# Matmul operands at the same place modulo 512 bytes of SBUF

## The chip, the cores and the metric

The kernel runs on one core of a Trainium2 chip. The metric is the time of one execution on the device, in microseconds (us).

## The reference

One layer of a streaming encoder over 512 tokens of 1024 features, in float32: a half ffn, a mixer with three attention branches, a second half ffn, and a last norm.

```python
x = x + 0.5 * swiglu(rmsnorm(x, ffn1_norm), ffn1_wg, ffn1_wu, ffn1_wd)      # D 1024, D_FF 2816
h = rmsnorm(x, mix_norm)
proj = h @ w_in                      # q, k, v of branches a and b, q of branch c
...                                  # a: differential attention, b: banded, c: into 256 memory tokens
gates = sigmoid(h @ w_gate + b_gate)
y = sum over branches of (o_i @ w_branch[i]) * gates[i]
x = x + y @ w_out
x = x + 0.5 * swiglu(rmsnorm(x, ffn2_norm), ffn2_wg, ffn2_wu, ffn2_wd)
x = rmsnorm(x, final_norm)
swiglu(h, wg, wu, wd) = (silu(h @ wg) * (h @ wu)) @ wd
```

## The kernel before

**Products in three terms.** Every large product is made of float32 operands that are split into a high and a low part of type fp32r (`split`, L75): ScalarE casts the high part (L77), VectorE subtracts (L78). A product is then three matmuls, high with high, high with low, low with high (`mm3`, L108, or `mm7`, L345). The names of the parts end in h and l, or hi and lo. A matmul has a stationary operand (lhsT, 128 columns of 512 bytes in each partition, loaded by a weight load of its own) and a moving one (rhs, 256, 384 or 512 columns). In the rows of the profile a matmul reads `ps_s<-mhi,whi`: it writes ps_s, its moving operand is mhi, its stationary one whi.

**The ffns.** The up products (`mm7`, L354) are made with seven combined products per pair of weight tiles in place of eight: the tokens are combined once into M1 to M7 (`Operands`, tiles mhi and mlo), the weight blocks are combined as they arrive (`Item.prep`). A product is 24 matmuls of 256 columns: M moving, a weight block stationary. Weight blocks stand in a ring of six (`block`, L339): four of them in whi and wlo, two in fhi and flo. The gated results stand in gh and gl. In the down products they are stationary and the weight blocks moving, 512 columns each (`mm3` at L110 to L112). `run_jobs` lays out the order of the products and of the weight blocks that are split ahead of them.

**The mixer.** h2 (hh and hl) is the normed input, transposed. In the units' projections (`proj_rows`, 384 columns) and in those of c and of the memory, it or the memory's mh and ml is stationary, and the weights move; in the gates (`gate`) the weights are stationary (fh and fl) and h2 moves, in the branches (`branch`) oT (oah, obh, och and their low parts) moves. The scores read qk and kx, the products with the probabilities read vt and pT. The order of the work on TensorE is written out by hand (the PLAN strings); a scheduler with a model of time orders the other engines.

**Places in SBUF.** Pools stack their tiles from the bottom of each partition up; pools with side="right" stack from the top down, which is at byte 229344, 480 bytes over a multiple of 512. The pool base lies below all others; its last tiles are many of 32 bytes (`tiny`), and the tile le of 32 bytes (L619). mhalf is 8 columns that hold -0.5, of which GpSimd reads at most the first four (L121). Nearly all operand tiles have a length that is a multiple of 512 bytes, so that the rest of a tile's place modulo 512 is that of all its slices of 128 columns. The rests of the operands that the large products read:

| product | matmuls, columns | moving | its rest before | stationary | its rest before | both after |
|---|---|---|---|---|---|---|
| ffns, up | 2496 x 256 | M (mhi, mlo) | 480 | whi, wlo | 32 | 32 |
| ffns, up | 1200 x 256 | M | 480 | fhi, flo | 64 | 32 |
| ffns, down | 720 x 512 | whi, wlo | 32 | gh, gl | 64 | 32 |
| ffns, down | 336 x 512 | fhi, flo | 64 | gh, gl | 64 | 32 |
| gates | 576 x 512 | hh, hl | 480 | fh, fl | 160 | 32 |
| branches | 288 x 512 | oah, obh, och, ... | 64 | fh, fl | 160 | 32 |
| units' projections | 768 x 384 | whi, wlo | 32 | hh, hl | 480 | 32 |
| projections of c | 96 x 512 | whi, wlo | 32 | hh, hl | 480 | 32 |
| projections of the memory | 96 x 512 | mwh, mwl | 64 | mh, ml | 480 | 32 |
| output product | 192 x 512 | whi, wlo, kx, w4 | 32 | yh, yl | 64 | 32 |
| scores of the units | 128 x 256 to 512 | qk, kx | 64, 32 | qk | 64 | 32 |

Of the kernel before, what the change touches and what calls it, by code (L numbers as in the profile page):

```python
# [11 lines left out]
F32 = mybir.dt.float32  # L12
# [6 lines left out]
P = 128  # L19
# [28 lines left out]
def layer_kernel(ctx: ExitStack, tc: tile.TileContext, a: dict, out: bass.AP):  # L48
    nc = tc.nc

    base = ctx.enter_context(tc.tile_pool(name="base", bufs=1))
# [19 lines left out]
    def buf4k(name):  # L71

        return base.tile([P, 1024], F32, tag="raw", name=name, bufs=6)
# [18 lines left out]
    def load(src, n):  # L92

        raw = buf4k("wraw")[:, :n]
        dst = raw
        if len(src.shape) == 3:
            dst = raw.rearrange("p (a b) -> p a b", a=src.shape[1])
        nc.sync.dma_start(out=dst, in_=src)
        return raw
# [30 lines left out]
    def load_gain(name):  # L130
        g = scratch("gain")
        nc.sync.dma_start(out=g, in_=a[name].partition_broadcast(P))
        return g[:, :512], g[:, 512:]
# [29 lines left out]
    def right_pool(name):  # L163
        return tc.tile_pool(name=name, bufs=1, side="right", reuse_waits="tile")
# [6 lines left out]
    def new_M(pool):  # L171
        mh, ml = (pool.tile([P, 7, 4, HS], F32R, name=n) for n in ("mhi", "mlo"))
        return {i: (mh[:, i - 1], ml[:, i - 1]) for i in range(1, 8)}
# [59 lines left out]
    def squares(src):  # L233
# [4 lines left out]
            square_half(src[:, d], dump[:, d], ss[:, dh:dh + 1])  # L238
        return ss

    Mp = right_pool("M1")
    M1 = new_M(Mp.__enter__())
    memp = tc.tile_pool(name="memp", bufs=1, reuse_waits="tile")
# [7 lines left out]
    for t in range(NT):  # L251
        nc.sync.dma_start(out=x_sb[:, t, :], in_=x_v[:, t, :])
        if t == 0:
            gain1 = load_gain("ffn1_norm")
        elif t < 3:
            w1_raw.append(load(a["ffn1_w1"][0, t - 1], 1024))

    ident = base.tile([P, P], F32, name="ident")
    make_identity(nc, ident)
# [2 lines left out]
    mhalf = base.tile([P, 8], F32, name="mhalf")  # L262
# [353 lines left out]
    nc.sync.dma_start(out=la, in_=a["a_lambda"].rearrange("(u v) d -> u v d", u=2).partition_broadcast(P))  # L616
    lp = heads(lam[:, 256:384], 2)
    nc.vector.tensor_tensor(out=lp, in0=la[:, :, 0, :], in1=la[:, :, 1, :], op=ALU.mult)
    le = base.tile([P, 4], F32, name="le")  # L619
    nc.vector.tensor_reduce(out=le[:, 0:2], in_=lp, axis=AX.X, op=ALU.add)  # L620
    nc.scalar.activation(out=le[:, 0:2], in_=le[:, 0:2], func=AF.Exp)
    nlam = le[:, 2:3]
# [14 lines left out]
    mo = mix_o.__enter__()  # L637
    mix = tc.tile_pool(name="mix", bufs=1, reuse_waits="tile")
    mp = mix.__enter__()


    def bcast(name, src, n):
# [485 lines left out]
```

## Time and profile before

| | |
|---|---|
| median of 3 runs | 1273.69 us (1273.66 to 2465.04) |
| the profiled execution | 1273.05 us, of which 1271.3 us from the first to the last instruction (the span) |
| granted TensorE clock, mean | 0.987 |
| TensorE matmuls (PE) | busy 1232.4 us, 97% of the span, 7808 instructions |
| weight loads (PEld) | busy 1116.9 us, 88%, 7808 |
| VectorE (DVE) | busy 842.8 us, 66% |
| ScalarE (ACT) | busy 596.8 us, 47% |
| GpSimd (POOL) | busy 107.1 us, 8% |
| read from HBM | 122.11 MB, 99 GB/s over the span |

The busy times are those of one execution. Matmuls overlap: one starts while the one before it is still in the array, so the duration of a matmul in a row (276 to 397 ns here) is longer than the distance between two starts. That distance is read from the starts in the timeline, or from a row of the chain that merges many matmuls of one kind.

### The profile page before, as it was taken

What the parts mean: (1) busy time and instruction counts of PE and PEld (TensorE: products, weight loads), DVE (VectorE), ACT (ScalarE), POOL (GpSimd) and SP (SyncE); (2) the same over time, 40 slices, a digit from 0 to 9 for tenths busy, and PEclk for the clock granted to TensorE, in tenths of its full rate; (3) what the DMA queues carried; (4) which work ended last, traced back from release to release, by engine and by line L of the source; (5) the groups of instructions that cost most, each with busy time, mean ns of one, the idle gap of its engine ahead of it and who ended that gap; (6) DMA issues with size and microseconds to landing.
All of it is one profiled execution on the core that took longest, in us unless ns stands there. A gap on an engine that the chain in (4) does not pass through costs nothing.

```text
span 1271.3 us, 19657 instructions
## 1 busy us (share of the span) xinstructions
PE 1232.4 (97%) x7808; PEld 1116.9 (88%) x7808; DVE 842.8 (66%) x1377; ACT 596.8 (47%) x1115; POOL 107.1 (8%) x108
## 2 busy tenths in 40 slices
PE   7799999999998999999999999999979999999997
PEld 7789989989986799999999999888878998998996
DVE  7977667667564756766765565453697766766753
ACT  7535425435443446554555454443463452543543
POOL 1100000000000301111221121020000000000002
PEclk8899999999999899999999999999989999999999
DMA  5533324322334403321222320254133242342311
GB/s 215 174 108 116 115 71 128 113 91 101 116 118 130 109 28 108 88 67 58 88 87 70 89 83 31 75 159 160 34 127 122 76 133 91 101 129 73 130 35 67
DMA packets 53084, 127.57 MB, mean 100 GB/s; under 512 B 10112, under 2 KB 10624, under 8 KB 52992
## 3 DMA queue, kind: packets, MB, share of 16 engines
q1 hardware_dynamic: 52416, 125.27, 30.9%
q8 instruction: 61, 1.00, 0.3%
q10 hardware_dynamic: 576, 1.05, 0.2%
q14 instruction: 31, 0.25, 0.1%
HBM read 122.11 MB, written 4.19 MB: 99 GB/s over the span
## 4 chain that ended last, share of the span: by engine, by line
PE 90%; DVE 4%; DMA 2%; ACT 1%; POOL 1%; issue 1%; SPq 0%; POOLq 0%; ACTq 0%; DVEq 0%
PE ps_s L354 19%; PE ps_g L110 9%; PE ps_g L112 9%; PE ps_g L111 9%; PE ps_o L354 5%; PE ps_p L110 4%; PE ps_p L354 4%; PE ps_p L111 4%; PE ps_p L112 4%; PE ps_g L354 4%; PE ps_s L110 2%; PE ps_s L112 2%; PE ps_s L111 2%; PE ps_o L881 2%; PE ps_s L849 2%; PE ps_t L697 1%
## 5 line engine op out<-in xcount | busy, mean ns | idle before, releaser
L77 ACT CAST whi<-wraw 128x1024 fp32r<-128x1024 f32 (+1 forms) x120 | 119.0, 993 | 141.3 <-PE ps_s L354 68.6
L78 DVE TENSOR_TENSOR wlo<-wraw,whi 128x1024 fp32r<-128x1024 f32 (+1 forms) x120 | 137.9, 1151 | 65.6 <-ACT whi L77 64.6
L354 PE MATMUL ps_s<-mhi,whi 128*128 128x256 f32 x496 | 138.3, 279 | 2.3 <-ACT snap L397 2.0
L354 PE MATMUL ps_s<-mlo,whi 128*128 128x256 f32 x496 | 137.7, 278 | 0.0
L354 PE MATMUL ps_s<-mhi,wlo 128*128 128x256 f32 x496 | 136.8, 278 | 0.0
L77 ACT CAST whi<-quarter 128x1024 fp32r<-128x1024 f32 x54 | 56.7, 1051 | 91.8 <-PE ps_s L354 22.7
L354 PEld LDWEIGHTS ps_s<-mhi,whi 128*128 128x128 f32 x496 | 93.8, 189 | 4.1 <-ACT snap L397 2.8
L110 PE MATMUL ps_p<-whi,hh 128*128 128x384 f32 (+1 forms) x264 | 94.8, 359 | 0.0
L354 PEld LDWEIGHTS ps_s<-mlo,whi 128*128 128x128 f32 x496 | 93.7, 189 | 1.0 <-DVE mlo L78 0.2
L354 PEld LDWEIGHTS ps_s<-mhi,wlo 128*128 128x128 f32 x496 | 93.2, 189 | 0.0
L112 PE MATMUL ps_p<-whi,hl 128*128 128x384 f32 (+1 forms) x264 | 89.2, 338 | 0.0
L111 PE MATMUL ps_p<-wlo,hh 128*128 128x384 f32 (+1 forms) x264 | 89.2, 338 | 0.0
L78 DVE TENSOR_TENSOR wlo<-quarter,whi 128x1024 fp32r<-128x1024 f32 x54 | 65.9, 1221 | 24.5 <-ACT whi L77 24.5
L110 PE MATMUL ps_g<-hh,fh 128*128 128x512 f32 x192 | 78.4, 408 | 0.0
L112 PE MATMUL ps_g<-hh,fl 128*128 128x512 f32 x192 | 75.8, 395 | 0.0
L111 PE MATMUL ps_g<-hl,fh 128*128 128x512 f32 x192 | 75.7, 394 | 0.0
L834 DVE CAST kx<-ps_t 128x256 fp32r<-128x256 f32 x32 | 13.6, 425 | 83.7 <-PE ps_t L832 83.7
L121 POOL TENSOR_TENSOR rsh<-msh,mhalf 128x4 f32<-128x4 f32 x38 | 45.2, 1191 | 276.9 <-DVE msh L127 225.2
L78 DVE TENSOR_TENSOR fl<-wraw,fh 128x768 fp32r<-128x768 f32 x48 | 50.0, 1042 | 26.1 <-ACT fh L77 26.1
L77 ACT CAST fhi<-quarter 128x1024 fp32r<-128x1024 f32 x34 | 35.5, 1049 | 59.1 <-PE ps_s L354 16.4
L354 PE MATMUL ps_s<-mhi,fhi 128*128 128x256 f32 x208 | 59.2, 285 | 2.5 <-ACT fhi L77 2.5
L354 PE MATMUL ps_s<-mlo,fhi 128*128 128x256 f32 x208 | 58.9, 283 | 0.0
(376 smaller groups left out, 3662.8 us busy)
## 6 DMA issues: line engine op xcount, KB each, us to landing
wraw<-in_ffn_w SPq DMA_DIRECT2D x88, 512.0 KB, 4.0
wraw<-in_ffn_wd SPq DMA_DIRECT2D x44, 512.0 KB, 3.9
wraw<-in_w_u SPq DMA_DIRECT2D x32, 384.0 KB, 3.3
wraw<-in_w_gb SPq DMA_DIRECT2D x32, 384.0 KB, 3.0
wraw<-in_w_gf SPq DMA_DIRECT2D x16, 384.0 KB, 3.1
wraw<-in_w_mem_kv SPq DMA_DIRECT2D x8, 512.0 KB, 4.1
wraw<-in_w_out SPq DMA_DIRECT2D x8, 512.0 KB, 4.5
x_sb<-in_x SPq DMA_DIRECT2D x4, 512.0 KB, 7.0
```

The costliest lines, as they stand in the source:

```text
L77: nc.scalar.copy(out=hi, in_=raw)
L78: (engine or nc.vector).tensor_tensor(out=lo, in0=raw, in1=f32(hi), op=ALU.subtract)
L110: nc.tensor.matmul(ps, lhsT=st[0], rhs=mv[0], start=first, stop=False)
L111: nc.tensor.matmul(ps, lhsT=st[0], rhs=mv[1], start=False, stop=False)
L112: return nc.tensor.matmul(ps, lhsT=st[1], rhs=mv[0], start=False, stop=last)
L121: nc.gpsimd.tensor_tensor(out=rs, in0=ms, in1=mhalf[:, :n], op=ALU.pow)
L354: nc.tensor.matmul(ps[:, c], lhsT=x, rhs=y, start=first and j + k + n == 0, stop=k == 3 and n == 2, skip_group_check=True)
L697: nc.tensor.transpose(ps[:, j * P:(j + 1) * P], pt[:, j * P:(j + 1) * P], ident)
L834: nc.vector.tensor_copy(out=un.kx[:, :, qs], in_=heads(p2[:, 0:256], 2))
L849: nc.tensor.matmul(out_, lhsT=q, rhs=k, start=j == 0, stop=j == 1)
L881: nc.tensor.matmul(o[:, vs], lhsT=pT[:, j * P:(j + 1) * P], rhs=un.v[:, j, vs], start=j == 0, stop=j == i)
```

## The change

Two pads and a merged tile move the places of tiles; nothing else changes. A pad of 112 words (448 bytes) at the top of the right side, entered before M1, lowers all tiles of that side by 448 bytes: their rest goes from 480 to 32. The tile le is now columns 4 to 8 of mhalf, which makes base shorter by 32 bytes: the rest of the tiles that stand above it goes from 64 to 32. A pad of 104 words (416 bytes) behind the small tables of the pool mix moves the tiles behind it (vt, the score tiles, fh and fl, pT and others) from 160 to 32. The empty lines of the diff do nothing.

```diff
+    ctx.enter_context(right_pool("pad")).tile([P, 112], F32, name="pad")
     Mp = right_pool("M1")
     M1 = new_M(Mp.__enter__())
...
     nc.vector.tensor_tensor(out=lp, in0=la[:, :, 0, :], in1=la[:, :, 1, :], op=ALU.mult)
-    le = base.tile([P, 4], F32, name="le")
+    le = mhalf[:, 4:8]
     nc.vector.tensor_reduce(out=le[:, 0:2], in_=lp, axis=AX.X, op=ALU.add)
...
     mp = mix.__enter__()
+
+
+    mp.tile([P, 104], F32, name="pad")
```

Engine by engine the built program has the same instructions in the same order, with the same waits on the same values; only the name le has become mhalf in its three writers and 16 readers. The tiles that stand below le in base (x_sb, the raw weights, ident, whi and wlo, w4 and kx) keep their places. In the after kernel all operands of the table have rest 32; the stationary operands of the transposes get rest 32 or 288, and ident, which moves in them, stays at 128.

## Rows read from the trace of the kernel before

**Rows 1.** The page, part 4: the chain of waits, shares of the span.

```profile
PE 90%; DVE 4%; DMA 2%; ACT 1%; POOL 1%; issue 1%; SPq 0%; POOLq 0%; ACTq 0%; DVEq 0%
```

**Rows 2.** Windows: us, busy us (instructions) of each engine, clock, DMA share, GB/s.

```profile
66.00:372.00 306.00, 305.19 (x2107) 281.20 (x2106) 212.62 (x255) 133.47 (x192) 1.65 (x3) 1.00 0.33 105
...
456.00:805.00 349.00, 348.72 (x2097) 318.91 (x2096) 221.94 (x610) 183.09 (x496) 60.63 (x59) 1.00 0.24 74
...
938.00:1190.00 252.00, 249.55 (x1762) 231.73 (x1761) 181.86 (x209) 107.89 (x147) 0.00 (x0) 1.00 0.35 111
```

**Rows 3.** The chain of waits in time: start us, us, what.

```profile
1025.43 2.88 PE ps_g L354 x24
1028.31 2.73 PE ps_s L354 x24
```

**Rows 4.** Timeline of PE, second ffn: first matmuls of two blocks.

```profile
1025.26 0.28 PE L354 MATMUL ps_g<-mhi,fhi 128*128 128x256 f32 x1
...
1028.14 0.28 PE L354 MATMUL ps_s<-mhi,whi 128*128 128x256 f32 x1
```

**Rows 5.** Timeline of all engines, second ffn: a matmul, the next weight load.

```profile
1025.98 0.28 PE L354 MATMUL ps_g<-mhi,fhi 128*128 128x256 f32 x1
1025.99 0.19 PEld L354 LDWEIGHTS ps_g<-mlo,fhi 128*128 128x128 f32 x1
```

**Rows 6.** Source L354, ffns, up: count, ns min/median/max, first and last start.

```profile
L354 PE MATMUL ps_s<-mhi,whi x496: 275/276/562, 16.4 to 1235.9; 128*128 128x256 f32 x166
...
L354 PE MATMUL ps_s<-mhi,fhi x208: 277/283/582, 40.5 to 1219.4; 128*128 128x256 f32 x104
```

**Rows 7.** Tile gh, ffns, down: the same columns.

```profile
L110 PE MATMUL ps_g<-whi,gh x120: 392/396/476, 66.2 to 1263.6; 128*128 128x512 f32 x120
...
L110 PE MATMUL ps_s<-fhi,gh x28: 387/390/504, 77.9 to 1239.9; 128*128 128x512 f32 x28
```

**Rows 8.** Timeline of PE, first ffn, down: from whi to fhi.

```profile
255.66 0.40 PE L112 MATMUL ps_o<-whi,gl 128*128 128x512 f32 x1
...
256.60 0.39 PE L110 MATMUL ps_s<-fhi,gh 128*128 128x512 f32 x1
...
258.66 0.39 PE L110 MATMUL ps_s<-fhi,gh 128*128 128x512 f32 x1
...
261.84 0.39 PE L112 MATMUL ps_p<-fhi,gl 128*128 128x512 f32 x1
```

**Rows 9.** Source L78, VectorE's subtraction in a split: columns as above.

```profile
L78 DVE TENSOR_TENSOR wlo<-quarter,whi x54: 1215/1220/1227, 39.3 to 1210.3; 128x1024 fp32r<-128x1024 f32 x54
...
L78 DVE TENSOR_TENSOR flo<-quarter,fhi x34: 1215/1224/1226, 43.0 to 1212.6; 128x1024 fp32r<-128x1024 f32 x34
```

**Rows 10.** Source L111, the third term of other products: columns as above.

```profile
L111 PE MATMUL ps_p<-wlo,hh x264: 332/336/398, 372.6 to 787.9; 128*128 128x384 f32 x128, 128*128 128x512 f32 x4
L111 PE MATMUL ps_g<-hl,fh x192: 387/395/399, 433.9 to 865.9; 128*128 128x512 f32 x192
...
L111 PE MATMUL ps_s<-mwl,mh x32: 391/394/629, 394.8 to 430.7; 128*128 128x512 f32 x32
...
L111 PE MATMUL ps_g<-oal,fh x32: 392/397/401, 644.4 to 791.4; 128*128 128x512 f32 x32
...
L111 PE MATMUL ps_s<-wlo,yh x16: 392/396/398, 846.7 to 910.8; 128*128 128x512 f32 x16
```

**Rows 11.** Waits of TensorE: waiter, awaited, us in total, times, longest.

```profile
PE ps_o L354 <- ACT whi L77: 7.3, 2, 3.7
PE ps_s L110 <- DVE mk L580: 5.6, 1, 5.6
```

**Rows 12.** Windows, one stretch at a lower clock: columns of rows 2.

```profile
412.72:419.54 6.82, 5.57 (x14) 4.33 (x15) 5.00 (x11) 1.19 (x2) 2.67 (x4) 0.50 0.33 113
```

**Rows 13.** Groups by shape, scores of the units: count, busy us, mean ns, idle.

```profile
L849 PE MATMUL ps_s<-qk 128*128 128x256 f32 x32 | 8.3, 281 | 0.0
...
L849 PE MATMUL ps_s<-qk 128*128 128x512 f32 x16 | 6.3, 394 | 0.0
```

## The prediction

> **What bounds the kernel now.** I read the page first. TensorE is busy for 97% of the span (the table above), and the chain of waits runs through it for 90% [rows 1]. The windows by stage show where: in the first ffn (66 to 372 us), the mixer (456 to 805 us) and most of the second ffn (938 to 1190 us) TensorE is busy for all but 0.3 to 2.5 us, while VectorE, the next engine, stands at 64 to 72% [rows 2]. In these stretches the time is the number of matmuls times the distance from one matmul's start to the next one's. I call that distance the pitch. So the question is what the pitch depends on.
>
> The chain of waits shows it. It merges each product of an ffn into one row of 24 matmuls. All these blocks do the same work, 256 moving columns of M against a weight block, yet some rows last 2.73 us and others 2.88 us [rows 3]. The timeline says which is which: the block of 2.88 us reads its weight block from fhi and flo, the next one, of 2.73 us, from whi and wlo [rows 4]. Per matmul that is 120 ns against 113.7 ns. The two kinds differ in nothing but the place of the stationary operand. M begins at rest 480 (modulo 512 bytes), whi at 32, fhi at 64.
>
> The timeline with both parts of TensorE says how one operand's place can touch the other: the load of the next matmul's weights starts 0.01 us after the running matmul does [rows 5]. So the two read SBUF side by side, from the matmul's first column on. The source view of that line gives the same difference as duration, median 276 ns with whi and 283 ns with fhi [rows 6].
>
> The down products of the ffns repeat it the other way round, with 512 moving columns and gh (rest 64) stationary. With whi moving (rest 32) the median is 396 ns, with fhi (rest 64, the same) 390 ns [rows 7]. The pitch agrees: 0.94 us for the last four matmuls of a run with whi, 235 ns, and 3.18 us for 14 in the run with fhi behind it, 227 ns [rows 8]. So fhi is the dear operand with M and the cheap one with gh. It is not the tile, but its place against its partner's. In the dear pairs the two rests differ by an odd multiple of 32 bytes (fhi and M, gh and whi, oT and fh); in the cheapest they are equal (gh and fhi) or 64 apart (whi and M). Pairs that are 192 apart (h2 and fh) stand between them, at 395 ns [rows 10].
>
> **The change part by part.** No instruction is added, removed or moved, and every wait stands where it stood, so nothing is queued differently on any engine or DMA queue. The pads hold no data and issue nothing: cost 0. The small tile le becomes four columns of mhalf; its three small writers and 16 readers are the same instructions, and GpSimd reads only the first columns of mhalf: cost 0.
>
> ScalarE, VectorE and GpSimd read and write the moved tiles too. The split of a weight block lasts a median 1220 ns into wlo (rest 32) and 1224 ns into flo (rest 64) [rows 9]. So I price their new places at 0; between bounds of 4 ns either way on some 400 splits that is at most 1.6 us, on engines that are not the bound.
>
> What is left is the pitch. I price each family at the difference between its present value and that of the one large family that has equal rests now, fhi with gh:
>
> - M with fhi: rows of 24 that fall from 2.88 to 2.73 us. There are 208 matmuls of M's high part with fhi into ps_s [rows 6] and 64 into each of three other banks, 400, and three terms of each: 1200, or 50 blocks. 50 x 0.15 = 7.5 us.
> - M with whi: 104 blocks, at 2.73 us already. Cost and gain 0.
> - whi with gh: 120 matmuls of the first term into ps_g [rows 7] and 120 into the other banks, times three terms, 720. 720 x 6 ns = 4.3 us.
> - h2 with fh (the gates): 576, median 395 ns to 390 ns [rows 7, 10]: 2.9 us.
> - oT with fh (the branches): 288, 397 to about 391 ns [rows 10]: 1.7 us.
> - whi with h2, 384 columns (the units' projections): 768, median 336 ns [rows 10]. No row has this shape with equal rests. Halfway between the cheap 276 and 390 ns of 256 and 512 columns lies 333 ns: 768 x 3 ns = 2.3 us. The bounds are 0 and 5 ns, so 0 to 3.8 us.
> - The output product: 192, 396 to 390 ns [rows 10]: 1.2 us.
> - The memory's and C's projections: 192, 394 to 390 ns [rows 10]: 0.8 us.
> - Scores, transposes and products with the probabilities are short bursts, and in the scores one of two operands has the partner's rest already: 0, between -1 and +1 us.
>
> The sum is 20.7 us. Nine tenths of these matmuls stand in the stretches in which TensorE is never idle; of the rest (start, memory stage, output product, tail) I count half. That takes off about 1.2 us and leaves 19.5 us. What is late next does not stop it: the largest wait of TensorE on another engine is 7.3 us in all [rows 11], and VectorE would need some 28% less TensorE time to become the bound. The profiled execution took 1273.05 us, 1271.3 of it span, and the median of the runs is 0.6 us above it. 1273.05 - 19.5 + 0.6 = 1254 us.
>
> The clock can move this by a few us. The granted share is 0.50, which is 1.2 of 2.4 GHz, in a few stretches; the one at 412.7 us [rows 12] comes after TensorE had waited 5.6 us for VectorE [rows 11]. TensorE was busy for 5.57 us in it, so at the full clock it would be at most 2.8 us shorter. One such stretch more or less is in the range.
>
> **The rivals.** (1) The places do not matter, and something else sets the two pitches, such as the region of SBUF in which whi and fhi lie. Then nothing changes: 1274 us. Against it: fhi is slow with M and fast with gh. For it: rests and regions were never varied apart in this trace. The Trainium skill, TensorE: Matmul & The Clock Gate, Step-by-step: what each phase is for, states that the moving operand and the weight load have independent read ports and that the load takes nothing from the running matmul; by that rule the sum is 0, and the rows of 2.73 and 2.88 us speak against it. Chance 12%.
>
> (2) Slower: equal rests are good for 512 columns only, the one length at which this trace shows them in long runs, and with 256 columns they are a worse place than the 64 bytes that M and whi have now. The scores have equal rests at 256 columns, and last a mean 281 ns there [rows 13], 5 ns over the median of M with whi. Against it: they are bursts of four, and their 512-column form stands at 394 ns [rows 13], 4 over the 390 of the long runs, so a burst seems to cost 4 to 5 ns whatever the length. If M went to 2.88 us a block, the 104 blocks with whi would cost 15.6 us, the 50 with fhi give nothing, and the other families still give 13.2: 1276 us. With the 4.5 ns of the bursts in place of 6.3, and 2 ns gained with fhi, it is 1269 us. It decides against the change from 5.6 ns per matmul of M on (20.7 us over 3696 matmuls). Chance 13%.
>
> (3) TensorE gets faster, and half of it is lost because the splits of ScalarE and VectorE then come too late for the next block: 1264 us. For it: the wait of 7.3 us on whi [rows 11]. Against it: both engines mostly wait for TensorE. Chance 9%.
>
> (4) Equal rests everywhere are better still than fhi with gh now, where the neighbouring blocks have other rests and the first matmuls of a run pay for the switch: in rows 8 from 256.60 to 258.66 us stand nine matmuls of 229 ns before the 227 set in. The least durations are 1 ns under the median with 256 columns [rows 6] and 3 ns under it with 512 [rows 7]. 3696 x 1 ns and 3072 x 3 ns (all the longer ones) give 13 us more: 1241 us. Chance 6%.
>
> **How the numbers follow.** My forecast, 1254 us, has 60%, with 1249 to 1260 us as its own range (the 384-column bounds, the small bursts and one clock stretch). The range over the cases runs from 1249 to 1272 us: it leaves out most of (4), most of (1) and part of (2), together about 20%. About 2% (25.5 us, below 1248.2 or above 1299.2) is what a measurement of this kernel can tell from no change. My sum lies inside that. Faster by more needs (4) or a clock stretch less on top of the whole sum: 9%. Slower by more needs 7 ns on every matmul of M and no gain elsewhere: 1%. Within 2%: 90%.
>
> **What would show it.** Right: no row of 24 matmuls at 2.88 us in the chain any more, all at 2.73; 283 to 276 ns for M with fhi; 396 to 390 ns for whi with gh; 336 to about 333 ns for the units' projections; the same waits. Wrong: M with whi above 2.73 us (rival 2), durations unchanged (rival 1), or durations down and a longer list of waits on TensorE (rival 3).

## The result, and the profile after

The changed kernel takes 1281.25 us (median of 4 runs, 1279.72 to 1282.67) against 1273.68 us of the kernel before beside it: a ratio of 1.0063, 95% interval [1.0051, 1.0075]. One run of the kernel before took 2465.04 us and is left out of the ratio. The changed kernel is 0.6% slower, where 1.5% faster was forecast, and lies above the range. The profiled execution's span is 1277.9 us (before 1271.3).

The page of the changed kernel, span and busy time of the engines: TensorE is busy 7.6 us longer than before (1232.4 us) with the same 7808 matmuls, and the chain still runs through it for 90%, as in [rows 1].

```profile
span 1277.9 us, 19657 instructions
...
PE 1240.0 (97%) x7808; PEld 1133.2 (89%) x7808; DVE 842.6 (66%) x1377; ACT 597.5 (47%) x1115; POOL 104.2 (8%) x108
...
PE 90%; DVE 4%; DMA 2%; ACT 2%; issue 1%; POOL 1%; SPq 0%; POOLq 0%; ACTq 0%; DVEq 0%
```

The windows of the stretches of [rows 2]: TensorE is as full as it was and its clock is 1.00 in all three, but it starts 21, 4 and 29 matmuls fewer in the same time. What grew is the time of a matmul in the ffns.

```profile
66.00:372.00 306.00, 304.88 (x2086) 284.26 (x2085) 208.98 (x248) 130.35 (x186) 1.10 (x2) 1.00 0.32 103
456.00:805.00 349.00, 348.76 (x2093) 319.49 (x2092) 221.24 (x610) 182.42 (x494) 60.88 (x59) 1.00 0.24 73
938.00:1190.00 252.00, 250.08 (x1733) 233.94 (x1732) 182.48 (x209) 107.52 (x146) 0.00 (x0) 1.00 0.35 112
```

The chain of waits in time, second ffn. Before, rows of 2.88 and of 2.73 us alternated [rows 3]; now rows of 24 without a wait have 2.87 or 2.88, 120 ns a matmul.

```profile
1008.89 2.88 PE ps_g L357 x24
...
1012.01 2.88 PE ps_s L357 x24
1014.89 2.88 PE ps_o L357 x24
```

The source view of the ffns' up line: M with whi went from a median 276 ns [rows 6] to 283, and M with fhi stayed at 283.

```profile
L357 PE MATMUL ps_s<-mhi,whi x496: 277/283/562, 16.3 to 1243.2; 128*128 128x256 f32 x166
...
L357 PE MATMUL ps_s<-mhi,fhi x208: 277/283/583, 40.3 to 1226.4; 128*128 128x256 f32 x104
```

The down products and the other products of the mixer did what was forecast of their durations: 396 to 389 ns [rows 7], 395, 394 and 397 to 389 or 390, 336 to 334 [rows 10].

```profile
L110 PE MATMUL ps_g<-whi,gh x120: 389/389/477, 66.7 to 1270.3; 128*128 128x512 f32 x120
```

```profile
L111 PE MATMUL ps_p<-wlo,hh x264: 331/334/397, 377.4 to 792.3; 128*128 128x384 f32 x128, 128*128 128x512 f32 x4
L111 PE MATMUL ps_g<-hl,fh x192: 387/389/398, 438.0 to 868.9; 128*128 128x512 f32 x192
...
L111 PE MATMUL ps_s<-mwl,mh x32: 387/389/628, 399.5 to 434.8; 128*128 128x512 f32 x32
...
L111 PE MATMUL ps_g<-oal,fh x32: 387/390/397, 648.4 to 795.9; 128*128 128x512 f32 x32
```

A duration has a modelled end, so I also took from both traces the distance from each matmul's start to the next one's (the pitch) and summed it by family. "Apart" is the rest of the stationary operand less that of the moving one, modulo 512 bytes; after, it is 0 for all.

| family (columns) | matmuls | apart, before | pitch ns, before to after | sum us, before to after |
|---|---|---|---|---|
| M with whi (256) | 2496 | 64 | 113.8 to 119.9 | 294.9 to 308.3 |
| M with fhi (256) | 1200 | 96 | 119.8 to 120.0 | 156.2 to 157.0 |
| whi with gh (512) | 720 | 32 | 233.2 to 227.3 | 168.2 to 163.7 |
| fhi with gh (512) | 336 | 0 | 228.2 to 227.7 | 79.0 to 79.3 |
| whi with h2 (384) | 768 | 448 | 173.5 to 175.3 | 139.2 to 140.5 |
| h2 with fh (512) | 576 | 192 | 231.3 to 230.0 | 137.1 to 135.7 |
| oT with fh (512) | 288 | 96 | 233.6 to 229.9 | 68.5 to 67.4 |
| whi with yT (512) | 192 | 32 | 233.2 to 226.8 | 44.9 to 43.6 |
| memory's and C's projections (512) | 192 | 416, 448 | 233.1 to 227.7, 230.0 to 228.9 | 53.4 to 52.8 |

(Pitches are means without the gaps in which TensorE waited; the sums hold those.) M costs 14.2 us more, the other families 7.3 us less, together 6.9 us; the span grew by 6.6.

### The profile page after: what moved, and what is told of

It reads as the page before. It is cut to its first block, busy times and chain, and to the rows that moved or that the text cites. A ratio compares the mean times of both kernels' runs of the same rounds, so it can differ in the third digit from the quotient of the medians.

```text
span 1277.9 us, 19657 instructions
## 1 busy us (share of the span) xinstructions
PE 1240.0 (97%) x7808; PEld 1133.2 (89%) x7808; DVE 842.6 (66%) x1377; ACT 597.5 (47%) x1115; POOL 104.2 (8%) x108
## 4 chain that ended last, share of the span: by engine, by line
PE 90%; DVE 4%; DMA 2%; ACT 2%; issue 1%; POOL 1%; SPq 0%; POOLq 0%; ACTq 0%; DVEq 0%
PE ps_s L357 19%; PE ps_g L110 9%; PE ps_g L112 9%; PE ps_g L111 9%; PE ps_o L357 5%; PE ps_p L357 5%; PE ps_p L110 4%; PE ps_p L112 4%; PE ps_p L111 4%; PE ps_g L357 4%; PE ps_s L110 2%; PE ps_s L111 2%; PE ps_s L112 2%; PE ps_o L887 2%; PE ps_s L855 2%; PE ps_t L703 1%
## 5 line engine op out<-in xcount | busy, mean ns | idle before, releaser
L78 DVE TENSOR_TENSOR wlo<-wraw,whi 128x1024 fp32r<-128x1024 f32 (+1 forms) x120 | 137.9, 1150 | 68.8 <-ACT whi L77 68.1
L357 PE MATMUL ps_s<-mhi,whi 128*128 128x256 f32 x496 | 141.3, 285 | 2.3 <-ACT snap L400 2.0
L357 PE MATMUL ps_s<-mlo,whi 128*128 128x256 f32 x496 | 140.8, 284 | 0.0
L357 PE MATMUL ps_s<-mhi,wlo 128*128 128x256 f32 x496 | 139.8, 284 | 0.0
L111 PE MATMUL ps_p<-wlo,hh 128*128 128x384 f32 (+1 forms) x264 | 89.1, 337 | 0.0
L78 DVE TENSOR_TENSOR wlo<-quarter,whi 128x1024 fp32r<-128x1024 f32 x54 | 65.9, 1220 | 29.2 <-ACT whi L77 29.2
L111 PE MATMUL ps_g<-hl,fh 128*128 128x512 f32 x192 | 74.9, 390 | 0.0
L78 DVE TENSOR_TENSOR fl<-wraw,fh 128x768 fp32r<-128x768 f32 x48 | 50.0, 1041 | 25.4 <-ACT fh L77 25.4
```

Of the source, the lines that this page charges most:

```text
L78: (engine or nc.vector).tensor_tensor(out=lo, in0=raw, in1=f32(hi), op=ALU.subtract)
L111: nc.tensor.matmul(ps, lhsT=st[0], rhs=mv[1], start=False, stop=False)
L357: nc.tensor.matmul(ps[:, c], lhsT=x, rhs=y, start=first and j + k + n == 0, stop=k == 3 and n == 2, skip_group_check=True)
```

## The experiments

My theory after the result: a load of weights and the running matmul disturb each other by the distance of their places, and at 256 columns equal rests are a dear distance (rival 2 of the prediction). Against it stood that absolute places or single tiles count, and that M is slow for what runs before it.

**1. M's pad left out, and M's pad alone.** The first kernel is the changed one without the pad of M, the second the kernel before with that pad and nothing else.

```
-    ctx.enter_context(right_pool("pad")).tile([P, 112], F32, name="pad")
```

> The change without its right pad: M, h2 and mT stay at rest 480, all else goes to 32. M then lies 64 before both whi and fhi, gh and the weights that move against it have equal rests. Theory distance (the pitch follows from the distance of the two rests and the number of columns; at 256 columns 64 apart is cheap and 0 dear): M with whi back to 113.5 ns a matmul, M with fhi down from 120 to 113.5 ns too, whi with gh 227 ns: about 1273.7 - 7.5 - 4.5 - 1.3 - 1.1 = 1259 us, between 1255 and 1262 since h2 with fh goes to 64 apart, which no row of 512 columns shows. Theory region (fhi is dear with M wherever it begins): M with fhi stays at 120 ns, 1267 us. Theory of equal rests that are good everywhere, with something else that made the changed kernel slow: no better than 1274 us.

```
+    ctx.enter_context(right_pool("pad")).tile([P, 112], F32, name="pad")
```

> The kernel before with the right pad alone: M at rest 32, whi at 32, fhi and gh at 64. Theory distance: M with whi (0 apart) at 120 ns as in the changed kernel, M with fhi now 32 apart, which is as dear as any odd multiple of 32 has been, 117 to 121 ns; whi with gh back at 233 ns. About 1273.7 + 13.4 + 0 to 1 = 1287 us. If the slowdown came from the two other edits, it is 1274 us or less.

The first took 1273.05 us, ratio 0.9998 [0.9988, 1.0008]; the second 1286.55 us in one run (1273.42 before). The pad of M is what costs: 8 us in the changed kernel, 13 us alone. But the first did not come to the sum of the gains, for which about 1259 us had been expected. Its source view of the up line has 281 ns for M with both weights, which are both 64 apart now as whi was before, at 276 [rows 6]:

```profile
L354 PE MATMUL ps_s<-mhi,whi x496: 275/281/562, 16.3 to 1237.7; 128*128 128x256 f32 x166
...
L354 PE MATMUL ps_s<-mhi,fhi x208: 276/281/581, 40.5 to 1221.1; 128*128 128x256 f32 x104
```

The pitch of M is 117.4 and 117.3 ns: fhi gained 2.5 ns and whi lost 3.6 without any change of its own places. That is a third value beside 113 and 120, and it had to be explained.

**2. Everything elsewhere, at the same distances.** The changed kernel without the mixer's pad, with 64 bytes of pad in the base pool: M at 32, the weights and gh at 96.

```
+    base.tile([P, 16], F32, name="bpad")
-    mp.tile([P, 104], F32, name="pad")
```

> M at rest 32 as in the changed kernel, but whi, fhi and gh 64 bytes higher, at 96 (without the pad of the mixer, for want of room). Theory distance: M lies 64 before its weights as before, so 113.5 ns with whi and with fhi, and 227 ns for whi with gh: the ffns as in the kernel without the right pad, about 1260 us; the branches (96 apart) stay at 234 ns. Theory place (M is cheap at rest 480 and dear at rest 32, whatever its partner): 120 ns for both, about 1282 us.

It took 1274.0 us in one run, where 1260 had been expected. M is at 117.2 and 117.1 ns and whi with gh at 226.8: every family is within 0.8 ns of the first kernel but oT with fh, which is 96 apart here (233.2, there 229.7). (h2 with fh has another distance too, 160 here and 64 there, and says nothing on this question.) For M and the ffns it is the distance that counts, not the place.

**3. Three other distances.** The changed kernel with a shorter pad of M, so that M is 256 (as in the diff), 128 (16 columns for 48) and 192 (32 columns) apart from its weights.

```
-    ctx.enter_context(right_pool("pad")).tile([P, 112], F32, name="pad")
+    ctx.enter_context(right_pool("pad")).tile([P, 48], F32, name="pad")
```

> The changed kernel with a right pad of 48 words in place of 112: M, h2 and mT at rest 288, 256 from their partners, with 256, 384 and 512 columns alike. Theory distance: if what counts repeats every 64 bytes or every 256, M costs 120 ns as at 0 apart, and the time is near the 1281 us of the changed kernel; if M was only dear where both start at the very same rest, 113.5 ns, and some 1259 us. h2 with fh and whi with h2 tell the same for 512 and 384 columns.

> The changed kernel with a right pad of 16 words: M, h2 and mT at rest 416, 128 from their partners; gh and its weights equal. 256 apart was the same as 0 apart in every family, so distances count at most modulo 256, and 128 is the one left between. Theory of distance with locks: a pitch of M that is some state of its own, 113.4 ns (then 1259 us) if 128 apart keeps the two streams clear of each other whatever came before, 117.8 to 120 ns (1273 to 1281 us) if it has a slow lock too. If distances counted modulo 128, M stands at 120 ns as at 0 and 256 apart.

> The changed kernel with the pad of M cut to 128 bytes: M stands at the rest of 352, 192 apart from its weights, the multiple of 64 that is not yet measured at 256 columns; the hidden side of the down products of h2 stands 192 apart too. If 192 acts like 64 (the same distance the other way round a circle of 256), M keeps a pitch of 113 or 117.8 ns and the time is 1258 to 1275 us. If only 64 is good, M stays at 120 ns: 1281 us, and h2 x fh goes to some 231 to 233 ns, 1281 to 1283 us.

256 apart it took 1280.32 us in one run, with M at 119.9 and 120.0 ns and every family within 0.2 ns of the changed kernel (the memory's projections 0.5), so places 256 bytes apart acted like equal ones. 128 apart it took 1282.18 us in one run, with M at 119.8, as dear. 192 apart it took 1275.63 us, ratio 1.0017 [1.0007, 1.0026], with M at 117.8. With M and fhi at 96 apart (119.8, before) and at 32 (118.2, the pad alone), the table of 256 columns is, as means over whole runs: 0, 96, 128 and 256 apart 120 ns; 32 and 192 apart 118; 64 apart 113.8 or 117.4. Equal rests are among the worst.

**4. The length.** The changed kernel with each down product of 512 columns made as two of 256.

```
+                        for j in range(2):
+                            c, oc_ = slice(j * HS, (j + 1) * HS), slice(o.start + j * HS, o.start + (j + 1) * HS)
...
+                                nc.tensor.matmul(acc[t][:, c], lhsT=x, rhs=y, start=k == 0 and j + n_ == 0,
+                                                 stop=k == nf - 1 and n_ == 2, skip_group_check=True)
```

> The changed kernel, in which each down product of 512 columns at equal rests is made as two of 256 columns (the same values, 1056 matmuls become 2112). Theory that equal rests are dear because a matmul has 256 columns: each half takes about 120 ns as the products of M do, 1056 x (240 - 227) ns more, about 1295 us. Rival, that M is dear for what it is (its tile, its weights) and not for its length: a half takes half of 226.7 ns, 113.4, and the time stays at about 1281 us.

It took 1295.79 us, ratio 1.0172 [1.0157, 1.0187], the number of the length theory. The source view of the halves shows M's 283 ns on quite other tiles, and the chain of waits 1.44 us for 12, 120 ns each:

```profile
L492 PE MATMUL ps_g<-whi,gh x240: 278/283/366, 66.8 to 1286.0; 128*128 128x256 f32 x120
```

```profile
999.93 1.44 PE ps_g L492 x12
```

So equal rests are good at 512 columns (227 against 233 ns) and bad at 256 (120 against 113 at best), whatever the tile.

**5. What ran before.** The first kernel has M at 117.4 ns where the kernel before, at the same distance from whi, has 113.8. The theory: at 64 apart two pitches hold themselves, and the matmuls ahead decide which one a run falls into. The chain of waits of the first kernel suggests it: with the same places a block of M lasts 2.72 us ahead of the first down products and 2.83 behind them.

```profile
55.71 2.72 PE ps_o L354 x24
...
72.16 2.83 PE ps_s L354 x24
```

The test is the first kernel with pads in the ffns' pool, so that gh stands 32 apart from its partners again, M unmoved:

```
+                fp.tile([P, 8], F32, name="gpad")
...
+                fp.tile([P, 120], F32, name="fpad")
```

> The kernel without the right pad (M at 480, whi and fhi at 32, 64 apart), with gh and gl moved by a pad to rest 64, so that the down products lie 32 apart again as whi and gh did before. M's own places are the same as in that kernel, where M ran at 117.8 ns a matmul from the first down product on. Theory entry (at 64 apart the weight loads can lock to the running matmul in two ways, 113.4 and 117.8 ns, and the matmuls ahead of a product decide which; down products at equal rests leave the slow one): M with whi and with fhi both 113.4 ns, the down products 233 ns; about 1273.4 - 7.8 (M with fhi) + 2 (fhi with gh) - 2 (output product, branches) = 1266 us. Theory pair (only the two operands of a product count): M stays at 117.8 ns as without the right pad, and with dearer down products it is 1279 us.

It took 1267.32 us in one run (1275.33 before), with M at 114.3 and 114.2 ns and the down products back at 233.2. Nothing of M's places differs from the first kernel. The down products come in 20 stretches. In the first kernel M settles at 117.8 ns behind all 20; here it settles at 113.3 behind 19, and at 117.8 behind one, for 432 matmuls from 984 us on. So down products 32 apart led to the short pitch nearly always, but not every time. The chain of waits shows the exception and its end in the second ffn: blocks of 2.83 us until the next down products at 1035 us, 2.75 for the block between them, 2.73 behind them.

```profile
984.58 2.83 PE ps_s L354 x24
...
1032.64 2.83 PE ps_o L354 x24
...
1037.79 2.75 PE ps_s L354 x24
...
1046.60 2.73 PE ps_s L354 x24
```

**6. A break of the rhythm alone.** The first kernel with one or three more matmuls of 256 columns (M moving, the identity as weights, 160 apart, result unread) behind each down product. They are extra work only. A first form asked for them ahead of M's next product:

```
+        def kick(v, n=1):
+            if after_down[0]:
+                ps = bank("t")
+                for _ in range(n):
+                    nc.tensor.matmul(ps[:, :HS], lhsT=identr, rhs=v[:, 0, :], start=True, stop=True)
+            after_down[0] = False
...
+            kick(M[m][0])
```

> The kernel without the right pad, with three more matmuls of 256 columns ahead of the first product of M behind each down product: M moving, identr stationary (rest 128, 160 behind M), their result is not read. All other operands and their places are the same. Theory entry: the three break the slow lock and M then runs at 113.4 ns; the down products stay at 227 ns: 1273 - 3696 x 4 ns + some 15 x 3 x 0.12 = 1264 us or a little less. Theory pair: M at 117.8 ns still, and the time is 1273 + 5 = 1278 us. If three matmuls at 160 lead to the slow lock as well, this reads like theory pair, and the run at a distance that has one lock alone has to tell.

> The same with one matmul ahead instead of three. Theory entry: where three break the lock, one may or may not; if it does, 1260 us, if not, 1275 us. The rows of the first matmuls behind it show how long the way into a lock is (3 to 4 matmuls behind M with fhi in the kernel before).

They took 1278.56 and 1274.70 us in one run each, with M at 117.3 to 117.5 ns, which is inconclusive. The extra matmuls depend on nothing but M, and the order of the program put them all at the start of the two ffns, none behind a down product; with three (source view of their line):

```profile
L351 PE MATMUL ps_t<-mhi,identr x48: 277/281/388, 26.8 to 934.4; 128*128 128x256 f32 x48
```

In the second form they stand behind the third matmul of M's first product after a down product (the call moves to the end of the loop over k in mm7), and spread over both ffns.

> The kernel without the pad of M (M 64 away from both its weights, everything in the ffns at equal rests), and behind the third matmul of the first product of M after each down product three more matmuls of 256 columns, with M as the moving operand and the identity as the weights (160 apart), whose result nothing reads. They are extra work only. Theory of two locks: at 64 apart the products of M hold either a pitch of 113.3 or one of 117.8 ns, and what ran before them decides which; a break of the rhythm behind the down products lets them fall into the short one, as the irregular blocks of the kernel before do. Then the 3696 matmuls of M cost some 4 ns less each, 15 us, of which the extra matmuls (8 x 3 of about 0.12) take 3: about 1260 us, with the down products still at 227 ns. Rival: the pitch belongs to the pair of kernels' places as a whole and not to what ran before, or this break is of the wrong kind: M stays at 117 to 118 and the time is 1273 to 1277 us.

> The same with one extra matmul instead of three behind each down product. Theory of two locks: one break can throw the rhythm to either lock, so 1258 us if it suffices, and between that and 1274 if it suffices after some of the down products alone. Rival (the break does nothing): M stays at 117 to 118 ns, 1273 to 1275 us.

With three it took 1266.46 us, ratio 0.9943 [0.9928, 0.9958]; with one 1262.72 us, ratio 0.9912 [0.9897, 0.9927], the best kernel of this study. M runs at 114.0 and 113.9, or 113.8 and 113.7 ns, the down products at 227.0. (There are 16 such places, not 8, one of them at the start of each ffn and 14 behind stretches of down products: 48 and 16 extra matmuls. The 32 that differ take 4.0 us in the traces; the medians differ by 3.7.) With one, M settles at 113.3 ns behind all 14 of these stretches, and at 117.8 behind the other six, which no extra matmul follows. In the chain of waits of the kernel with one, the block at 1035.44 stands between two parts of a down product, without an extra matmul, and takes 2.83 us. The next one starts at 118 ns (three in 0.36 us), meets the extra matmul on ps_t, and its other 21 take 2.38 us, 113.3 each; so do the 24 behind it.

```profile
1035.44 2.83 PE ps_s L363 x24
...
1044.16 0.36 PE ps_s L363 x3
1044.51 0.12 PE ps_t L351
1044.63 2.38 PE ps_s L363 x21
1047.02 2.72 PE ps_o L363 x24
```

**7. The same break at equal rests.** Was the changed kernel's 120 ns also only what its down products left behind? The one extra matmul at the same points of the order, in the changed kernel and in the one with M 192 apart. (As M has moved, the extra matmul's own operands are 96 and 288 apart here, not 160.)

> The changed kernel itself, all equal rests, with the one extra matmul behind each down product (M moving, the identity as weights). Theory of two locks at 64 apart and a single one at equal rests: there is no short lock to fall into here, so M stays at 120 ns and the time at 1281 us, or 1 us more. Rival, that the changed kernel is slow only because its regular down products hold M in the long lock, and equal rests have a short one too: M goes to some 113.5 ns, 3696 x 6.4 = 24 us less, about 1258 us.

> The changed kernel with M 192 apart from its weights (1275.6 us, M at 117.8 ns without the extra matmul) and one extra matmul behind each down product. If 192 apart is 64 apart the other way round, with both locks, M goes to 113 to 114 ns and the time to 1261 to 1265 us. If 192 apart has the long lock alone, M stays at 117.8 ns, 1275 to 1277 us.

The changed kernel took 1283.60 us, ratio 1.0081 [1.0066, 1.0096], with M at 119.9 and 120.0 ns; the one with M 192 apart took 1278.10 us, ratio 1.0040 [1.0026, 1.0054], with M at 117.7 and 117.8. Both kept their mean pitch and paid for the 16 matmuls. The source view of the up line at equal rests:

```profile
L366 PE MATMUL ps_s<-mhi,whi x496: 277/283/562, 16.3 to 1248.0; 128*128 128x256 f32 x166
```

This break finds no shorter pitch at equal rests: no 20 distances of M in a row average below 119 ns in this run. It leads to none at 192 apart either, but there the same trace shows that one exists. At the start of the second ffn, ahead of the extra matmul, 33 distances in a row take 3.74 us, 113.3 ns each, at a granted clock of 1.00 (timeline):

```profile
917.33 0.28 PE L364 MATMUL ps_s<-mlo,whi 128*128 128x256 f32 x1
...
921.07 0.28 PE L364 MATMUL ps_g<-mhi,wlo 128*128 128x256 f32 x1
```

Behind the transposes that follow, M is back at 117.8. So two pitches are not peculiar to 64 apart, and what leads to the short one at 192 was not found.

## Why the prediction was wrong

**The step that failed** is the price: "I price each family at the difference between its present value and that of the one large family that has equal rests now, fhi with gh". That family has 512 columns. M has 256, and there equal rests are dear.

- "M with fhi: rows of 24 that fall from 2.88 to 2.73 us", -7.5 us: they stayed at 2.88, +0.8 us. M went from one dear distance, 96, to another, 0. The 2.73 us were not a price of equal rests at all: they were read from M with whi, 64 apart, a distance that the change takes away.
- "M with whi: 104 blocks, at 2.73 us already. Cost and gain 0": they rose to 2.88, +13.4 us. I wrote that I priced against equal rests and did not ask what leaving 64 apart costs. Experiments 1, 3 and 4 show both steps wrong from one cause.
- whi with gh, -4.3: right, -4.5. The output product, -1.2: right, -1.3. oT with fh, -1.7: -1.1. The memory's and C's projections, -0.8: -0.6.
- h2 with fh, -2.9: mis-sized, -1.4. The median duration fell from 395 to 389 ns as forecast, but the mean pitch from 231.3 to only 230.0. In the trace these matmuls stand in short pieces between scores and projections, and after each switch the first ones have starts mostly 228 to 237 ns apart before 227 sets in. The prediction had read such a switch in [rows 8] and used it only for rival 4.
- whi with h2 at 384 columns, -2.3 with bounds of 0 and -3.8: outside them, +1.3 us. Pitch 173.5 to 175.3 ns, though the median duration of the third term fell from 336 to 334: the duration was the wrong row to price from. The first kernel of experiment 1, with 448 apart kept there, has 173.8.
- "Nine tenths of these matmuls" stand in the full stretches: in the trace of the kernel before it is 5140 of 6768 in the stretches of [rows 2], three quarters. By the prediction's own halving that takes off some 3 us in place of 1.2; it is not what failed.
- "The same waits" and no cost of the pads: right. TensorE's longest wait is 7.5 us in all, 7.3 before [rows 11].

**Rival 2** (13%) named the mechanism, and the places M with whi at 2.88 and M with fhi unchanged. Its 1276 us is 5 below the result, because it left the other families all of their 13.2 us, and they gave 7.3. The argument against it was that the 281 ns of the scores' 256-column form [rows 13] come from their being bursts of four. That could not decide it: the scores that read kx have 281 ns 32 apart, before, and 282 at equal rests, after, so these durations hardly tell the distances apart. The long runs of M do, at 283 in the changed kernel.

```profile
L849 PE MATMUL ps_s<-kx,qk 128*128 128x256 f32 x32 | 8.3, 281 | 0.0
```

```profile
L855 PE MATMUL ps_s<-kx,qk 128*128 128x256 f32 x32 | 8.3, 282 | 0.0
```

**Rival 1** (places do not matter) falls with experiments 1 to 3. The rule of the Trainium skill beside it, TensorE: Matmul & The Clock Gate, Step-by-step: what each phase is for, that the weight load takes nothing from the running matmul's reads, does not fit these runs: with TensorE busy throughout, M with whi goes from 113.8 ns at 64 apart to 119.9 at equal rests. That the two reads disturb each other is the reading that fits; no view shows the reads themselves.

**What the prediction passed over** is that 2.73 us was no property of the pair M and whi. It sorted the rows into 2.73 us for whi and 2.88 for fhi, but the chain of waits of the kernel before also has fhi at 2.81 us (191.04) and whi at 2.83 (965.77):

```profile
191.04 2.81 PE ps_g L354 x24
...
965.77 2.83 PE ps_s L354 x24
```

The kernel before has 113.3 ns behind 15 of the 16 stretches of down products that M with whi follows. The kernel without M's pad makes the down products better and M worse, and comes out even (experiments 1, 5 and 6). Moving gh back to 32 apart was enough to restore the short pitch nearly always (experiment 5); what part the blocks on fhi had in the kernel before was not varied by itself. Why stretches with down products 32 apart lead to the short pitch, and stretches at equal rests throughout to the long one, is not settled: the runs show that they do, with one exception in each of the two kernels with gh 32 apart from whi, and that a single extra matmul is enough.

## What to carry to other kernels

Where TensorE is the bound, read the start-to-start distance of the matmuls by pair of operands and by number of columns, and price a move of an operand only from rows of the same length; the best distance of places at 512 columns was among the worst at 256. If the same pair shows two distances in one trace, look at what runs ahead of it: here one extra matmul behind 14 of the 20 stretches of down products made the kernel without M's pad 10 us faster and put it 0.9% ahead of the kernel before, more than any placement that was tried.

## What the runs showed of the hardware

- At the full clock (granted 1.00, 2.4 GHz) four of the pitches that long runs hold are whole multiples of 16 cycles above the columns: 113.3 ns is 272 cycles for 256 columns, 120 is 288; 226.7 is 544 for 512 columns, 233.3 is 560. The fifth, 117.8 ns at 256 columns, is 283 cycles and does not fit. The Trainium skill, TensorE: Matmul & The Clock Gate, Back-to-back issue gap, gives 262 cycles for 256 columns in isolation; no long run of 256 columns here came below 272.
- At 256 columns and 64 apart two pitches hold themselves for hundreds of matmuls, 113.3 and about 117.8 ns. One extra matmul of 119 ns moved TensorE from the second to the first, and down products at equal rests (227) moved it back. At 192 apart both were seen as well, 113.3 ns for 33 distances.
- Places 256 bytes apart acted like equal ones: M at 256 apart had every pitch of M at equal rests within 0.2 ns, as had h2 with fh and whi with h2.
